# Expert weights of a mixture-of-experts layer loaded in 16 KB runs per partition, with strided column reads on the other side

## The chip, the cores and the metric

The kernel runs on one core of a Trainium2 chip. The metric is the device time of one execution in microseconds (us), taken as the median of several runs. A core has five engines with instruction queues of their own: PE (TensorE, matrix products; PEld is its weight load, which runs beside the products), DVE (VectorE), ACT (ScalarE), POOL (GpSimd) and SP (SyncE, which here issues DMAs). Sixteen DMA engines carry data between HBM and the on-chip memory SBUF, which has 128 partitions.

## The reference

Two transformer blocks in fp32 on 256 tokens of width 1024. The first block has a mixer (RWKV-7 heads and block attention), then a mixture of 32 experts with top 4 of 32; the second block has attention, a projection and a dense feed-forward. What matters here is the expert layer of the first block:

```
logits = h @ w_router + b_router            # h = rms_norm(x, norm2_g) * (1 + scale2) + shift2
top_val, top_idx = lax.top_k(logits, 4);  weights = softmax(top_val)
for each expert e and the tokens that chose it (xb = h[tok]):
    gu   = xb @ w_gate_up[e] + b_gate_up[e]             # 1024 x 2048
    gate = min(gu[:, :1024], 7);  up = clip(gu[:, 1024:], -7, 7)
    act  = (up + 1) * gate * sigmoid(1.702 * gate)
    y    = act @ w_down[e] + b_down[e]                  # 1024 x 1024
x = x + gate2 * (sum over the experts of weight * y)
```

Each expert has 8 MB of w_gate_up and 4 MB of w_down, all of it read once: 32 x 12 MB.

## The kernel before, in words

The kernel has three stages. **Stage one** (`phase1`, L249) computes the conditioning rows (w_ada), the mixer, w_out and the router. Near its end `choose` (L913) transposes the residual `xm` in 128-column slices (L922), multiplies it by the router's weights `wr` (already scaled by `sc2` at L629) and finds each token's four experts. **Stage two** (`experts`, L1064) goes through the 32 experts. **Stage three** (`phase3`, L1250) is the second block.

In stage two an expert takes at most 64 tokens. Experts go in pairs: `gather` (L1091) builds one-hot matrices `s` for two experts and multiplies them with `xm`, eight slices of 128 columns by two halves of the tokens (L1108, the slice of `xm` is the stationary operand, which PEld loads); the result, scaled and shifted by columns of `sc2` and `sh2`, is `xe`, the gathered tokens with the model dimension on the partitions. `gate_up` (L1129) multiplies `xe` by the weights, `down` (L1151) transposes the activations in four 128-column slices (L1157, the slice of `act` is the stationary operand) and multiplies them by w_down; `combine` (L1173) adds the pair to the residual. PE runs the operations of this stage in the written order (class `InOrder`), so a gather of the next pair stands between gate_up and down of an odd expert.

The weights come as chunks of 2 MB, six per expert (`issue`, L1046): four of w_gate_up (two blocks of 128 rows each, of 2048 floats) and two of w_down (four blocks of 128 rows, of 1024 floats). Row p of a block goes to partition p:

```
g = A["w_gate_up"][e].rearrange("(k p) f -> p k f", p=128)
w = self.stream(g[:, 2 * j:2 * j + 2], 2, 2048, pool)
```

so a partition's part of a w_gate_up chunk is two runs of 8 KB, and of a w_down chunk four runs of 4 KB. All chunks are issued on SP's queue in order. There are nine slots of 16 KB per partition for them (`self.slots`); SP waits for the slot's last reader on PE and then issues. The first nine chunks are issued during stage one, which ends while they land. The last chunk of all is issued as four pieces of 512 KB.

The columns that `gather`, `choose` and `down` slice must match the rows that a partition holds: slice k of `xm` has the model dimensions that partition p of block k multiplies. `sc2` (from norm2_g, which comes with the small vectors at the start, and the conditioning rows through `ada_col`, L314), `sh2` and `wr` have the same order. For the last expert `cuts` (L1125) divides the work between gate_up and down into two halves of 256 columns, so that the first half's transposes start early. A branch for experts with more than 64 tokens (`overflow`, L973) is not taken with these inputs.

Of the kernel before, what the change touches and what calls it, by code (L numbers as in the profile page):

```python
# [88 lines left out]


CST_A, CST_B = _consts()


class InOrder:
# [20 lines left out]
class Kernel:  # L115
# [133 lines left out]
    def phase1(self):  # L249
# [61 lines left out]
            PE.matmul(ps, self.k("ones"), gacc[:, q], start=True, stop=True)  # L311
            return ps

        def ada_col(r, i0):  # L314

            ps = self.psum("adac")
            for j in range(4):
                PE.matmul(ps[:, 4 * j:4 * j + 4], r[:, j * 128:(j + 1) * 128], self.k("sel32")[:, i0:i0 + 4], start=True,
                          stop=True, skip_group_check=True)
            return ps[:, 0:16].rearrange("p (j i) -> p i j", i=4)  # L320

# [292 lines left out]

        wr = p1.tile([128, 8, NE], F32, tag="wr", name="wr")
        cvec = self.W[:, 0]
        with tc.issue_after(self.last_dma):
            nc.sync.dma_start(wr, A["w_router"].rearrange("(k p) e -> p k e", p=128))
            nc.sync.dma_start(cvec, A["b_router"].partition_broadcast(128))
        pv = ada_col(r1, 6)  # L620
        sc2, sh2 = self.sc2, self.sh2
        DVE.tensor_scalar(ic(sc2), pv[:, 2:4], 1.0, None, op0=OP.add)
        DVE.tensor_tensor(sc2, sc2, self.v("g2"), op=OP.mult)
        DVE.tensor_copy(ic(sh2), pv[:, 0:2])
        ps = self.psum("cv")
        for k in range(8):
# [286 lines left out]
    def choose(self, a, wrs, cvec):  # L913

        nc = self.nc
        PE, ACT, DVE = nc.tensor, nc.scalar, nc.vector
        x1, rs, ident, pr = self.xm, self.rs, self.k("ident"), self.prp
        x1T = pr.tile([128, 8, 128], F32, tag=f"x1T{a}", name="x1T")
        for k in range(0, 8, 4):
            ps = self.psum("x1t", chain=k > 3)  # L920
            for kk in range(4):
                PE.transpose(ps[:, kk * 128:(kk + 1) * 128], x1[:, a, (k + kk) * 128:(k + kk + 1) * 128], ident)  # L922
            o = ps.rearrange("p (a b) -> p a b", a=4)
            if k:
                ACT.activation(x1T[:, k:k + 4], o, AF.Copy)
            else:
                DVE.tensor_copy(x1T[:, k:k + 4], o)
        mask = self.mask[:, a]
        ps = self.psum("lg")
        for k in range(8):  # L930
            PE.matmul(ps[:, 0:NE], x1T[:, k], wrs[:, k], start=k == 0, stop=k == 7)
        lg = pr.tile([128, NE], F32, tag=f"lg{a}", name="lg")
        DVE.scalar_tensor_tensor(lg, ps[:, 0:NE], rs[:, a:a + 1], cvec, op0=OP.mult, op1=OP.add)
        m8 = pr.tile([128, 8], F32, tag=f"m8{a}", name="m8")
        DVE.max(m8, lg)
        ng = pr.tile([128, 2], F32, tag=f"ng{a}", name="ng")
        DVE.tensor_scalar(ng[:, 0:1], m8[:, 0:1], -1.0, None, op0=OP.mult)
        DVE.memset(m8[:, 4:8], BIG)
        zap = pr.tile([128, NE], F32, tag=f"zap{a}", name="zap")
        DVE.match_replace(zap, m8, lg, -BIG)  # L940
        DVE.tensor_tensor(mask, lg, zap, op=OP.not_equal)
        self.lgs = getattr(self, "lgs", []) + [(lg, ng)]
# [30 lines left out]
    def overflow(self):  # L973
# [4 lines left out]
        with tc.If(self.most > CAP):  # L978
            with tc.tile_pool(name="pof", bufs=1) as pool:
# [3 lines left out]
                with tc.For_i(0, NE, 1) as e:  # L983
# [5 lines left out]
                    def turned(normed):  # L989
                        for k in range(8):  # L990
                            ps = self.psum("ot")
                            PE.transpose(ps[:, 0:128], act[:, k * 128:(k + 1) * 128], ident)
                            if normed:
                                DVE.tensor_scalar(t8[:, k], ps[:, 0:128], self.sc2[:, k:k + 1], self.sh2[:, k:k + 1],
                                                  op0=OP.mult, op1=OP.add)
                            else:
                                DVE.tensor_copy(t8[:, k], ps[:, 0:128])
# [6 lines left out]
                    for a in range(2):  # L1004
                        DVE.tensor_scalar(act, xm[:, a], self.rs[:, a:a + 1], None, op0=OP.mult)
                        turned(True)
                        for i in range(2):
                            pg = [self.psum("og") for _ in range(2)]
                            for k in range(8):
                                for j in range(2):  # L1010
                                    c = slice(j * D + i * 512, j * D + (i + 1) * 512)
                                    w = weights("w_gate_up", slice(k * 128, (k + 1) * 128), c)
                                    PE.matmul(pg[j], t8[:, k], w, start=k == 0, stop=k == 7)
                            b = pool.tile([128, 2, 512], F32, tag="b", name="bo")
                            for j in range(2):
                                c = slice(j * D + i * 512, j * D + (i + 1) * 512)
                                nc.sync.dma_start(b[:, j], A["b_gate_up"][ds(e, 1), c].partition_broadcast(128))
                            g, u, s = b[:, 0], b[:, 1], act[:, i * 512:(i + 1) * 512]
                            DVE.tensor_tensor(g, pg[0], g, op=OP.add)
                            DVE.tensor_scalar(g, g, 7.0, None, op0=OP.min)  # L1020
                            DVE.tensor_tensor(u, pg[1], u, op=OP.add)
                            DVE.tensor_scalar(u, u, 7.0, -7.0, op0=OP.min, op1=OP.max)
                            ACT.activation(s, g, AF.Sigmoid, scale=1.702)
                            DVE.scalar_tensor_tensor(u, u, 1.0, g, op0=OP.add, op1=OP.mult)
                            DVE.tensor_tensor(s, s, u, op=OP.mult)
                        turned(False)
                        py = [self.psum("oy") for _ in range(2)]
                        for k in range(8):
                            for i in range(2):
                                w = weights("w_down", slice(k * 128, (k + 1) * 128), slice(i * 512, (i + 1) * 512))  # L1030
                                PE.matmul(py[i], t8[:, k], w, start=k == 0, stop=k == 7)
                        for i in range(2):
                            hs = slice(i * 512, (i + 1) * 512)
                            y = pool.tile([128, 512], F32, tag="y", name="oyy")
                            DVE.scalar_tensor_tensor(y, py[i], we[:, a:a + 1], self.gate2[:, hs], op0=OP.mult,
                                                     op1=OP.mult)
                            DVE.tensor_tensor(x1[:, a, hs], x1[:, a, hs], y, op=OP.add)
# [8 lines left out]
    def issue(self, upto):  # L1046

        A = self.A
        while self.issued < min(upto, 6 * self.ne):
# [2 lines left out]

            pool = self.slot(i, lambda p: e < self.ne - 1 or p is not self.ring)
            if j < 4:
                g = A["w_gate_up"][e].rearrange("(k p) f -> p k f", p=128)
                w = self.stream(g[:, 2 * j:2 * j + 2], 2, 2048, pool)
            else:
                d = A["w_down"][e].rearrange("(k p) f -> p k f", p=128)
                w = self.stream(d[:, 4 * j - 16:4 * j - 12], 4, 1024, pool, 4 if i == 6 * self.ne - 1 else 1)
            self.chunks[i] = w  # L1060
            self.issued += 1
            self.last_chunk = self.last_dma
# [1 line left out]
    def experts(self):  # L1064
# [26 lines left out]
        def gather(e):  # L1091
# [12 lines left out]
            for kk in range(0, 8, 4):  # L1104
                ps = self.psum("ga")
                for k in range(4):
                    for a in range(2):
                        PE.matmul(ps[:, k * 128:(k + 1) * 128], xm[:, a, (kk + k) * 128:(kk + k + 1) * 128], s[:, a],  # L1108
                                  start=a == 0, stop=a == 1, skip_group_check=True)
                for k in range(4):  # L1110
                    g, b = self.sc2[:, kk + k:kk + k + 1], self.sh2[:, kk + k:kk + k + 1]
# [12 lines left out]

        def cuts(e):  # L1125

            return [slice(0, 256), slice(256, 512)] if e == ne - 1 else [slice(0, 512)]

        def gate_up(e, ws):  # L1129
            xe = st[e & ~1][0][:, :, 64 * (e & 1):64 * (e & 1) + 64]  # L1130
# [11 lines left out]
                        PE.matmul(p[64 * h:64 * h + 64, :], xe[:, k], w[:, k % 2, c:c + 512], start=False, stop=k == 7)  # L1142
            u, s = (pool.tile([128, 512], F32, tag=n, name=n, bufs=1) for n in ("u", "sg"))
            for c in cuts(e):
                ACT.activation(s[:, c], pg[:, c], AF.Sigmoid, scale=1.702)  # L1145
                DVE.tensor_scalar(u[:, c], pu[:, c], 8.0, -6.0, op0=OP.min, op1=OP.max)  # L1146
                DVE.scalar_tensor_tensor(u[:, c], pg[:, c], 7.0, u[:, c], op0=OP.min, op1=OP.mult)
                DVE.scalar_tensor_tensor(u[:, c], s[:, c], SIG_MAX, u[:, c], op0=OP.min, op1=OP.mult)
            return u

        def down(e, act, ws):  # L1151
            at = pool.tile([128, 4, 2, 64], F32, tag="at", name="at")
            for c in cuts(e):
                ps = self.psum("at")
                js = slice(c.start // 128, c.stop // 128)
                for j in range(js.start, js.stop):
                    PE.transpose(ps[:, j * 128:(j + 1) * 128], act[:, j * 128:(j + 1) * 128], ident)  # L1157
                ACT.activation(at[:, js], ps[:, c].rearrange("p (j h s) -> p j h s", h=2, s=64), AF.Copy)  # L1158
            py = self.psum("py")
            for c in range(2):  # L1160
                for j in range(4):
# [446 lines left out]
```

## Time and profile before

| | us |
|---|---|
| median of 3 runs | 1568.0 (1567.0 to 1577.03) |
| the profiled execution | 1568.55 |
| its span, first to last instruction | 1566.8 |
| PE busy in the span | 1414.5 (90%) |
| DMA: bytes, mean rate | 505.15 MB, 322 GB/s |

The profiled execution is 0.55 us above the median. Its own time is 1.75 us more than its span; the rows below are all of that execution, with times in us from the start of the span. A busy PE is not a PE at its peak: a chunk's products come late when its data comes late. The page cuts the span into 40 slices of 39 us. Stage one fills the first seven of them, stage two ends in the 32nd, and stage three takes the rest.

### The profile page before, as it was taken

The page shows a single profiled execution, that of the slowest core. Times are in us where ns is not written, and L with a number is a line of the kernel's source. Part 1 is how long each engine was busy: PE and PEld are TensorE (multiplying, and loading weights), DVE is VectorE, ACT ScalarE, POOL GpSimd, SP SyncE. Part 2 cuts the span into 40 slices and gives each one's busy share as a digit, 9 for nine tenths or more (in the row PEclk, how much of TensorE's full clock was granted, in tenths as well). Part 3 has the DMA queues.
Part 4 walks back from the last instruction along what each step waited for, and adds up shares of the span by engine and source line. Part 5 has one row for each costly group of instructions (what it writes and reads, how often), then busy time and mean ns, then how long its engine had stood idle before and what let it go on. Part 6 is the DMA issues. An engine that isn't in the chain of part 4 may idle for free. (4 is left out here: it accounts for less than half of the span.)

```text
span 1566.8 us, 19105 instructions
## 1 busy us (share of the span) xinstructions
PE 1414.5 (90%) x7818; PEld 804.6 (51%) x7818; DVE 572.1 (37%) x1145; ACT 394.5 (25%) x767; POOL 212.9 (14%) x190
## 2 busy tenths in 40 slices
PE   5999999899999988888788889999888899899996
PEld 2976777433343333233233234433332597699995
DVE  3575877313122221122122122221211345565445
ACT  4862335101010000000010011100100366455553
POOL 1243661000000000000000000000000233252221
PEclk9998999899999999999999999999999999999998
DMA  9734747899999999999999999999999741525440
GB/s 335 262 118 148 265 166 285 339 419 415 418 418 416 416 418 417 416 417 419 416 416 418 416 413 416 417 418 416 418 417 417 285 162 54 215 108 202 175 162 28
DMA packets 115061, 505.15 MB, mean 322 GB/s; under 512 B 5548, under 2 KB 6572, under 8 KB 82168
## 3 DMA queue, kind: packets, MB, share of 16 engines
q1 hardware_dynamic: 114792, 503.74, 80.9%
q8 instruction: 63, 1.03, 0.3%
q14 instruction: 30, 0.25, 0.0%
q0 software_dynamic: 176, 0.14, 0.0%
HBM read 502.81 MB, written 1.05 MB: 322 GB/s over the span
## 5 line engine op out<-in xcount | busy, mean ns | idle before, releaser
L109 PE MATMUL pg<-w,xe 128*64 128x512 f32 x1024 | 271.2, 600 | 65.9 <-DMA w<-w_gate_up 65.9
L109 PE MATMUL pu<-w,xe 128*64 128x512 f32 x1024 | 267.5, 592 | 0.0
L109 PE MATMUL py<-w,at 128*64 128x512 f32 x1024 | 232.1, 606 | 23.1 <-ACT at L1158 20.6
L1146 DVE TENSOR_SCALAR u<-pu 128x512 f32<-128x512 f32 (+1 forms) x33 | 22.2, 675 | 477.0 <-PE pu L109 477.0
L1145 ACT ACTIVATE sg<-pg 128x512 f32<-128x512 f32 (+1 forms) x33 | 19.3, 584 | 690.7 <-PE pg L109 689.0
L109 PEld LDWEIGHTS pg<-w,xe 128*64 128x64 f32 x1024 | 70.0, 137 | 217.5 <-issue 112.0
L109 PEld LDWEIGHTS py<-w,at 128*64 128x64 f32 x1024 | 72.3, 139 | 161.6 <-issue 133.3
L109 PEld LDWEIGHTS pu<-w,xe 128*64 128x64 f32 x1024 | 75.5, 137 | 145.8 <-issue 145.6
L140 ACT ACTIVATE w3h<-w 128x512 fp32r<-128x512 f32 x184 | 115.4, 631 | 110.8 <-PE d L1299 59.4
L141 DVE TENSOR_TENSOR w3l<-w,w3h 128x512 fp32r<-128x512 f32 x132 | 96.8, 739 | 113.3 <-ACT w3h L140 108.5
L141 POOL TENSOR_TENSOR w3l<-w,w3h 128x512 fp32r<-128x512 f32 x52 | 67.3, 1299 | 430.4 <-ACT w3h L140 419.2
L1170 DVE TENSOR_TENSOR y<-py,gate 64x512 f32<-64x512 f32 x64 | 44.1, 689 | 209.4 <-PE py L109 208.7
L1298 PE MATMUL d<-xh,w3h 128*128 128x256 f32 x352 | 100.3, 287 | 0.9 <-ACT xh L1285 0.9
L1299 PE MATMUL d<-xl,w3h 128*128 128x256 f32 x352 | 100.8, 287 | 0.1
L1300 PE MATMUL d<-xh,w3l 128*128 128x256 f32 x352 | 100.5, 287 | 0.0
L1234 POOL TENSOR_TENSOR wml<-w,wml 128x512 fp32r<-128x512 f32 x4 | 5.1, 1278 | 695.1 <-ACT wml L1233 695.1
L1298 PEld LDWEIGHTS d<-xh,w3h 128*128 128x128 f32 x352 | 68.6, 196 | 1.6 <-ACT xh L1285 1.3
L1299 PEld LDWEIGHTS d<-xl,w3h 128*128 128x128 f32 x352 | 68.8, 195 | 0.6 <-DVE xl L1287 0.4
L1300 PEld LDWEIGHTS d<-xh,w3l 128*128 128x128 f32 x352 | 68.6, 195 | 0.2 <-DVE w3l L141 0.2
L109 PEld LDWEIGHTS ga<-s,xm 128*128 128x128 f32 x512 | 60.5, 197 | 13.5 <-issue 11.9
L109 PE MATMUL ga<-s,xm 128*128 128x128 f32 x512 | 63.6, 284 | 1.2 <-DVE s L1098 1.2
L109 PE MATMUL cb<-y,swt 128*128 128x512 f32 x128 | 59.2, 605 | 0.8 <-DVE y L1170 0.8
(421 smaller groups left out, 2041.1 us busy)
## 6 DMA issues: line engine op xcount, KB each, us to landing
w<-w_gate_up SPq DMA_DIRECT2D x128, 2048.0 KB, 24.9
w<-w_down SPq DMA_DIRECT2D x71, 2048.0 KB, 30.6
w<-w_ada SPq DMA_DIRECT2D x12, 2048.0 KB, 8.2
w<-w_up SPq DMA_DIRECT2D x8, 2048.0 KB, 7.6
w<-w_in SPq DMA_DIRECT2D x6, 2048.0 KB, 13.1
w<-w_in_sb SPq DMA_DIRECT2D x5, 2048.0 KB, 11.7
w<-w_out SPq DMA_DIRECT2D x4, 2048.0 KB, 7.7
w<-w_mem_kv SPq DMA_DIRECT2D x1, 2048.0 KB, 31.5
```

What stands on the lines that cost most here:

```text
L109: return self._keep(self.tc.nc.tensor.matmul(*a, **k))
L140: self.nc.scalar.activation(hi, src, AF.Copy)
L141: eng.tensor_tensor(lo, src, hi.bitcast(F32), op=OP.subtract)
L1145: ACT.activation(s[:, c], pg[:, c], AF.Sigmoid, scale=1.702)
L1146: DVE.tensor_scalar(u[:, c], pu[:, c], 8.0, -6.0, op0=OP.min, op1=OP.max)
L1170: DVE.tensor_tensor(st[e & ~1][2][r, hs], py[64 * h:64 * h + 64], self.gate2[64 * h:64 * h + 64, hs], op=OP.mult)
L1234: (POOL if k % 2 else DVE).tensor_tensor(wl, w[:, k], wh.bitcast(F32), op=OP.subtract)
L1298: PE.matmul(o, wh[:, ws], xh[:, k], start=k == 0 and i % 2 == 0, stop=False, skip_group_check=True)
L1299: PE.matmul(o, wh[:, ws], xl[:, k], start=False, stop=False, skip_group_check=True)
L1300: PE.matmul(o, wl[:, ws], xh[:, k], start=False, stop=k == 7, skip_group_check=True)
```

## The change: which row of the weights goes to which partition

Each partition now takes consecutive rows: two rows of w_gate_up (16 KB in one run) or four rows of w_down (16 KB in one run). The tokens' columns keep their order in SBUF. Slice k of the model dimension therefore becomes every second column of a 256-column block (`by_run`), and slice j of the activations every fourth column of a 512-column block; gather, the router's transposes and the transposes of the activations read these strided columns. norm2_g and w_router are loaded in the same order by four small DMAs each, on SP's queue behind the last conditioning weights, where one DMA of w_router stood; norm2_g goes straight into `sc2`, so that two DVE operations become one. The halves of the last expert become strided too. The last chunk still comes in four pieces of one row per partition.

```diff
+def by_run(k):
+    return slice(256 * (k // 2) + k % 2, 256 * (k // 2) + 256, 2)
...
-        def ada_col(r, i0):
+        def ada_col(r, i0, cols=lambda j: slice(j * 128, (j + 1) * 128)):
...
-                PE.matmul(ps[:, 4 * j:4 * j + 4], r[:, j * 128:(j + 1) * 128], self.k("sel32")[:, i0:i0 + 4], start=True,
+                PE.matmul(ps[:, 4 * j:4 * j + 4], r[:, cols(j)], self.k("sel32")[:, i0:i0 + 4], start=True,
...
+        sc2, sh2 = self.sc2, self.sh2
         with tc.issue_after(self.last_dma):
-            nc.sync.dma_start(wr, A["w_router"].rearrange("(k p) e -> p k e", p=128))
+            for c in range(4):
+                r = slice(256 * c, 256 * c + 256)
+                nc.sync.dma_start(wr[:, 2 * c:2 * c + 2], A["w_router"][r].rearrange("(p k) e -> p k e", k=2))
+                nc.sync.dma_start(sc2[:, 2 * c:2 * c + 2], A["norm2_g"][r].rearrange("(p k) -> p k", k=2))
             nc.sync.dma_start(cvec, A["b_router"].partition_broadcast(128))
-        pv = ada_col(r1, 6)
-        sc2, sh2 = self.sc2, self.sh2
-        DVE.tensor_scalar(ic(sc2), pv[:, 2:4], 1.0, None, op0=OP.add)
-        DVE.tensor_tensor(sc2, sc2, self.v("g2"), op=OP.mult)
+        pv = ada_col(r1, 6, by_run)
+        DVE.scalar_tensor_tensor(ic(sc2), pv[:, 2:4], 1.0, ic(sc2), op0=OP.add, op1=OP.mult)
...
-                PE.transpose(ps[:, kk * 128:(kk + 1) * 128], x1[:, a, (k + kk) * 128:(k + kk + 1) * 128], ident)
+                PE.transpose(ps[:, kk * 128:(kk + 1) * 128], x1[:, a, by_run(k + kk)], ident)
...
-                g = A["w_gate_up"][e].rearrange("(k p) f -> p k f", p=128)
-                w = self.stream(g[:, 2 * j:2 * j + 2], 2, 2048, pool)
+                g = A["w_gate_up"][e][256 * j:256 * (j + 1)].rearrange("(p k) f -> p k f", k=2)
+                w = self.stream(g, 2, 2048, pool)
             else:
-                d = A["w_down"][e].rearrange("(k p) f -> p k f", p=128)
-                w = self.stream(d[:, 4 * j - 16:4 * j - 12], 4, 1024, pool, 4 if i == 6 * self.ne - 1 else 1)
+                d = A["w_down"][e][512 * (j - 4):512 * (j - 3)].rearrange("(p k) f -> p k f", k=4)
+                w = self.stream(d, 4, 1024, pool, 4 if i == 6 * self.ne - 1 else 1)
...
-                        PE.matmul(ps[:, k * 128:(k + 1) * 128], xm[:, a, (kk + k) * 128:(kk + k + 1) * 128], s[:, a],
+                        PE.matmul(ps[:, k * 128:(k + 1) * 128], xm[:, a, by_run(kk + k)], s[:, a],
...
-            return [slice(0, 256), slice(256, 512)] if e == ne - 1 else [slice(0, 512)]
+            return [slice(0, 2), slice(2, 4)] if e == ne - 1 else [slice(0, 4)]
+        cut = lambda t, c: t.rearrange("p (q j) -> p q j", j=4)[:, :, c] if c != slice(0, 4) else t
...
-                ACT.activation(s[:, c], pg[:, c], AF.Sigmoid, scale=1.702)
+                ACT.activation(cut(s, c), cut(pg, c), AF.Sigmoid, scale=1.702)
...
-                    PE.transpose(ps[:, j * 128:(j + 1) * 128], act[:, j * 128:(j + 1) * 128], ident)
+                    PE.transpose(ps[:, j * 128:(j + 1) * 128], act[:, j:512:4], ident)
```

The three DVE operations behind the sigmoid take `cut` in the same way, and the branch that is not taken reads its rows and columns in the new order.

## Rows read from the trace of the kernel before

**Rows 1.** The page's slices: TensorE's clock, DMA busy share in tenths, and GB/s.
```profile
PEclk9998999899999999999999999999999999999998
DMA  9734747899999999999999999999999741525440
GB/s 335 262 118 148 265 166 285 339 419 415 418 418 416 416 418 417 416 417 419 416 416 418 416 413 416 417 418 416 418 417 417 285 162 54 215 108 202 175 162 28
```

**Rows 2.** Stretches: length, engines' busy us (instructions), TensorE's clock, DMA share, GB/s.
```profile
284.00:292.00 8.00, 8.00 (x46) 3.46 (x46) 4.21 (x14) 2.47 (x4) 0.00 (x0) 1.00 0.24 69
292.00:300.00 8.00, 7.49 (x36) 2.23 (x32) 0.45 (x1) 0.60 (x1) 0.00 (x0) 1.00 1.00 403
300.00:1180.00 880.00, 793.47 (x3836) 313.55 (x3838) 193.74 (x394) 73.99 (x154) 5.11 (x4) 0.99 1.02 417
1220.00:1228.00 8.00, 7.56 (x30) 2.51 (x30) 0.51 (x2) 0.77 (x2) 0.00 (x0) 0.79 1.04 392
```

**Rows 3.** Waits from 300 to 1225: us in total, times, longest us.
```profile
PE pg L109 <- DMA w<-w_gate_up: 65.9, 59, 1.7
PE py L109 <- ACT at L1158: 20.6, 30, 0.7
```

**Rows 4.** PE in order of time: start, us, operation, [idle before it <- what ended that].
```profile
560.96 0.65 PE L109 MATMUL pg<-w,xe 128*64 128x512 f32 x2 [0.43 <-DMA w<-w_gate_up]
...
621.11 1.08 PE L109 MATMUL pg<-w,xe 128*64 128x512 f32 x4 [0.41 <-DMA w<-w_gate_up]
...
626.08 0.65 PE L109 MATMUL pg<-w,xe 128*64 128x512 f32 x2 [1.32 <-DMA w<-w_gate_up]
...
863.62 1.08 PE L109 MATMUL pg<-w,xe 128*64 128x512 f32 x4 [0.41 <-DMA w<-w_gate_up]
...
868.59 0.65 PE L109 MATMUL pg<-w,xe 128*64 128x512 f32 x2 [1.32 <-DMA w<-w_gate_up]
```

**Rows 5.** Chunks issued about 1209: issue ns, first and last start; then landing times.
```profile
L133 SPq DMA_DIRECT2D w<-w_in_sb x2: 1767/5627/9487, 1209.6 to 1211.4; - x2
L133 SPq DMA_DIRECT2D w<-w_down x1: 4237/4237/4237, 1205.2 to 1205.2; - x1
...
DMA to landing us min/median/max: 19.3/20.3/23.8
```

**Rows 6.** The page's weight loads and products of all gathers: busy us, mean ns.
```profile
L109 PEld LDWEIGHTS ga<-s,xm 128*128 128x128 f32 x512 | 60.5, 197 | 13.5 <-issue 11.9
L109 PE MATMUL ga<-s,xm 128*128 128x128 f32 x512 | 63.6, 284 | 1.2 <-DVE s L1098 1.2
```

**Rows 7.** PEld from 300 to 1225: the transposes' loads of the activations.
```profile
L112 PEld LDWEIGHTS at<-ca,u 128*128 128x128 f32 x128 | 15.3, 141 | 14.4 <-DVE u L1148 7.5 <-issue 7.0
```

**Rows 8.** PE in order of time: a router transpose, the first gather, a later one.
```profile
270.09 0.65 PE L922 MATMUL x1t<-ca,xm 128*128 128x128 f32 x4
...
278.75 5.88 PE L109 MATMUL ga<-s,xm 128*128 128x128 f32 x32 [1.22 <-DVE s L1098]
...
604.57 3.84 PE L109 MATMUL ga<-s,xm 128*128 128x128 f32 x32
```

**Rows 9.** SP's queue in order of time, from 176 to 195.
```profile
176.68 0.58 SPq L618 DMA_DIRECT2D wr<-w_router  x1
177.31 3.08 SPq L619 DMA_DIRECT2D W<-b_router  x1
189.98 0.37 SPq L133 DMA_DIRECT2D w<-w_out  x1
```

**Rows 10.** PE's products with w_out's weights: ns min/median/max, first and last start us.
```profile
L877 PE MATMUL wo<-wsh,yoh x32: 389/389/501, 236.3 to 265.6; 128*128 128x512 f32 x32
```

**Rows 11.** The router's constant row, from 172 to 200 in order of time.
```profile
186.34 1.97 PE L627 MATMUL cv<-wr,sh 128*128 128x32 f32 x16
```

**Rows 12.** ACT and DVE about the last expert, in order of time.
```profile
1217.19 0.38 ACT L1145 ACTIVATE sg<-pg 128x256 f32<-128x256 f32 x1 [24.55 <-PE pg L109]
...
1218.79 0.42 DVE L1147 SCALAR_TENSOR_TENSOR u<-pg,u 128x256 f32<-128x256 f32 x1
```

More of the change, by code (lines that the diff above doesn't have):

```diff
@@ L991, in turned @@
                             ps = self.psum("ot")
-                            PE.transpose(ps[:, 0:128], act[:, k * 128:(k + 1) * 128], ident)
+                            c = by_run(k) if normed else slice(k * 128, (k + 1) * 128)
+                            PE.transpose(ps[:, 0:128], act[:, c], ident)
                             if normed:
@@ L1011, in overflow @@
                                     c = slice(j * D + i * 512, j * D + (i + 1) * 512)
-                                    w = weights("w_gate_up", slice(k * 128, (k + 1) * 128), c)
+                                    w = weights("w_gate_up", by_run(k), c)
                                     PE.matmul(pg[j], t8[:, k], w, start=k == 0, stop=k == 7)
@@ L1144, in gate_up @@
             for c in cuts(e):
-                ACT.activation(s[:, c], pg[:, c], AF.Sigmoid, scale=1.702)
-                DVE.tensor_scalar(u[:, c], pu[:, c], 8.0, -6.0, op0=OP.min, op1=OP.max)
-                DVE.scalar_tensor_tensor(u[:, c], pg[:, c], 7.0, u[:, c], op0=OP.min, op1=OP.mult)
-                DVE.scalar_tensor_tensor(u[:, c], s[:, c], SIG_MAX, u[:, c], op0=OP.min, op1=OP.mult)
+                ACT.activation(cut(s, c), cut(pg, c), AF.Sigmoid, scale=1.702)
+                DVE.tensor_scalar(cut(u, c), cut(pu, c), 8.0, -6.0, op0=OP.min, op1=OP.max)
+                DVE.scalar_tensor_tensor(cut(u, c), cut(pg, c), 7.0, cut(u, c), op0=OP.min, op1=OP.mult)
+                DVE.scalar_tensor_tensor(cut(u, c), cut(s, c), SIG_MAX, cut(u, c), op0=OP.min, op1=OP.mult)
             return u
@@ L1154, in down @@
                 ps = self.psum("at")
-                js = slice(c.start // 128, c.stop // 128)
-                for j in range(js.start, js.stop):
-                    PE.transpose(ps[:, j * 128:(j + 1) * 128], act[:, j * 128:(j + 1) * 128], ident)
-                ACT.activation(at[:, js], ps[:, c].rearrange("p (j h s) -> p j h s", h=2, s=64), AF.Copy)
+                for j in range(c.start, c.stop):
+                    PE.transpose(ps[:, j * 128:(j + 1) * 128], act[:, j:512:4], ident)
+                ACT.activation(at[:, c], ps[:, c.start * 128:c.stop * 128].rearrange("p (j h s) -> p j h s", h=2, s=64),
+                               AF.Copy)
             py = self.psum("py")
```

## The prediction, made before the changed kernel was run

> **What bounds the kernel now.** I read the page's slices first. The DMA engines are full from the ninth slice to the 31st, at 413 to 419 GB/s, and nowhere else for long [rows 1]. That is stage two. The stretches say the same: 417 GB/s and a DMA share of 1.02 over 880 us, while PE, though busy 793 of 880, waits [rows 2]. For what it waits stands in the table of waits: 65.9 us for w_gate_up [rows 3]. So stage two lasts as long as its weights take to come in, and PE has some 66 us to spare in it.
>
> Where does this stretch begin? At 284 to 292 the DMA engines stand nearly idle (69 GB/s), at 292 to 300 they are full [rows 2]. The nine slots hold the first nine chunks, and the tenth goes out when PE has used the first. So what delays the end of stage one delays everything; from there to the last chunk the time is the sum of the chunks' transfers; behind it comes a tail and stage three, which the change leaves alone.
>
> What does one chunk take? PE's waits for w_gate_up end when a chunk has landed. Two successive chunks: 621.11 and 626.08, or 863.62 and 868.59; both times 4.97 us [rows 4]. From 560.96 to 621.11 are two experts, 60.15 us, so 30.08 for one [rows 4]. Less four chunks of w_gate_up (19.88) that leaves 10.20 for two of w_down: **5.10 us**. (Ten experts, 560.96 to 863.62, give 30.27 each: now and then something else comes between; I leave that as it is.) Both chunks are 2 MB, so the difference lies in how the bytes are cut: 16 runs of 8 KB for each of the 16 DMA engines against 32 of 4 KB. A third point lies behind the stage: two chunks of w_in_sb, in runs of 2 KB (64 per engine), issued at 1209.6 and 1211.4, landed 20.3 and 23.8 us later (the 19.3 of that view is a piece of w_down), at 1229.9 and 1235.2: 5.3 us [rows 5]. The three lie near one line: (5.10 - 4.97)/16 = 8.1 ns per run, and (5.3 - 5.1)/32 = 6 ns with an error of some 3.
>
> **The change part by part.**
>
> *Runs of 16 KB.* Each engine then has 8 runs per chunk. No row shows weights in such runs. On the line a chunk takes 4.97 - 8 x 0.0081 = 4.905 us. The lower bound is the line's value at no cost per run, 4.97 - 16 x 0.0081 = 4.84; the upper bound, with no gain beyond 8 KB, is 4.97. I take the line: it holds from 2 KB to 8 KB, and 16 KB is one more step of the same kind. After the ninth chunk there are 183 in the full stretch: 121 of w_gate_up, 62 of w_down, of which the last still comes in pieces of 4 KB. The gain is 121 x 0.065 + 61 x 0.195 = 7.9 + 11.9 = **19.8 us**; between the bounds, 121 x 0 + 61 x 0.13 = 7.9 and 121 x 0.13 + 61 x 0.26 = 31.6. It is on the path in full as long as PE still waits: 65.9 less 19.8 leaves 46 us of waiting. What is late next is then the same chunk, earlier. SP isn't in the way: it issues a chunk some 20 us ahead of its landing [rows 5].
>
> The Trainium skill (DMA: Bandwidth & Descriptors, Why small descriptors are slow) speaks against this part: it gives a fixed cost of about three cycles per packet, which it says matters at 256 bytes or less. With its 850 MHz that is 3.5 ns per run, and the sum by it would be 121 x 8 x 3.5 ns + 61 x 24 x 3.5 ns = 8.5 us of gain, an estimate; the rows show more than twice its price per run, and I go by the rows.
>
> *Strided slices in gather.* The stationary operand `xm` is read with a step of 8 bytes. No PE operand of the kernel before that I cost here has a step, so the nearest rows are the same loads without one: 197 ns for a load of 128 columns by its record, and 3.84 us for the 32 products of one gather, 0.12 us per load and product [rows 6, 8]. Bounds per load: nothing (the load runs beside the product before it), and one more 0.12 if loads take twice as long. A gain is excluded, since a strided read fetches no less. I take nothing, the value of the rows as they are. In the full stretch, 480 of the 512 loads of gathers [rows 6] have PE's waits as cover; at 0.12 they would add 57.6 us and eat the 46 that are left. The first gather (5.88 us [rows 8]) has no cover: up to 32 x 0.12 = 3.8 us.
>
> *Transposes in choose.* 16 loads, four in 0.65 us [rows 8], on the way to the first gather: nothing, or 16 x 0.12 = 1.9 us.
>
> *Transposes of the activations.* 128 loads of 141 ns [rows 7], now with a step of 16 bytes: nothing, or 0.14 each; 124 of them under PE's waits (17.4 us at most), the last expert's four in the tail (0.6 us at most). Here the Trainium skill (SBUF — State Buffer, Door 1) has a rule that fits: a line of SBUF is 16 bytes and needs two hits for full rate, so a step of two fp32 is free and a step of four is not. By it only these loads grow, under cover, and the sum keeps its value but for the tail's 0.6; no run so far shows a strided load.
>
> *The last expert's halves.* ACT and DVE read and write 128x256 in pairs with a step: two halves of four operations, about 0.4 us each [rows 12], some ten with the copies, in a row behind the last w_gate_up chunk. Nothing at least, 4 us if each doubles. I take 0.3: the same elements in the same number of operations.
>
> *The small loads in stage one.* One DMA of w_router (0.58 us to issue) becomes eight. Between 0.37 and 0.58 each [rows 9], that is 2.4 to 4.1 us more on SP's queue. Behind them stand b_router (to 180.39) and then w_out at 189.98, which waits for its slot: 9.6 us of cover [rows 9]. If each took b_router's 3.08, w_out would go out 14 us late; its first product is at 236.3 [rows 10]. On PE the row `cv` needs the whole of `wr`, at 186.34 [rows 11]; what comes 2.4 to 4.1 us later there can hold up PE, and with it the products of the solve queued behind. `sc2` now waits for norm2_g as well, and DVE with it, if the order written out puts it early; the fused operation saves 0.16 us off the path. Bounds: nothing, and 4 us. I take 1, as most of the 4 is covered.
>
> **Sum.** 1568.55 (the profiled execution) - 19.8 + 0.3 + 1.0 = 1550.05. The median of the runs is 0.55 below that execution, so the forecast is **1549.5**.
>
> **The rivals.**
>
> *No step beyond 8 KB.* Either a 16 KB run is cut again on its way, or the per-run cost of the rows belongs to runs under 8 KB. Then w_gate_up stays at 4.97 and w_down falls to it: 7.9 us, less 1.3 of costs: 1568.0 - 6.6 = **1561.4**. For it: only three sizes lie on the line, and the third only roughly. Against it: from 4 to 8 KB the slope had not bent. The skill's price per packet, named above, ends at 1568.0 - 8.5 + 1.3 = 1560.8, an estimate, and so beside this case.
>
> *PE becomes the bound: slower.* A strided load takes longer than PE can hide. Place: the 480 loads of the gathers and 124 of the transposes in the full stretch, and 48 (first gather and choose) ahead of it. With x us more per load, the change is -19.8 + 1.3 + 48x + (604x - 46 if positive); it crosses zero at 652x = 64.5, x = 0.099 us. At 0.12 (loads twice as long, by the gather's pace) it is +13.7, **1582**; at the load's own 0.19 [rows 6], +59, 1627. For it: the pace of a gather is that of its loads, so nothing but PE's waits hides them. Against it: a step of 8 bytes is the smallest there is, and it would have to double.
>
> *Hidden anyway.* The gain comes in, but stage one loses as much as its bounds allow (4 + 3.8 + 1.9) and the tail 4: 1568.0 - 19.8 + 13.7 = 1562. It needs all four ends at once and is the least likely of these.
>
> **How the numbers follow.** A measurement of this kernel can tell about 1% from no change, here 15.7 us: below 1552.3 is faster, above 1583.7 slower. The line: 0.62, with its own range of 1538 to 1556 (gain of 31.6 to about 14), of which I put 0.52 under 1552.3 and 0.10 above. No step beyond 8 KB: 0.20. PE the bound: 0.12, of which 0.09 ends beyond 1%. Hidden anyway: 0.06. So faster 0.52; same 0.10 + 0.20 + 0.03 + 0.06 = 0.39; slower 0.09. The range reaches from 1541 over the second case to 1565: it leaves out the PE case (0.12) and the outermost of the line's low end (0.04).
>
> **What would show it.** Successive waits for w_gate_up end 4.90 us apart and two experts take 58.9 (12 x 4.905) instead of 60.15; 428 GB/s in the full stretch; half as many packets, and PE waiting some 46 us for w_gate_up. Chunks of w_gate_up still at 4.97 speak for the second case; PE's wait near nothing, with gathers over 5 us, for the third. The forecast is wrong at its root if chunks of 16 KB runs take longer than 5.01, the mean of the two kinds now: then runs of this length cost, which no row excludes.

## The result, and the profile after

The changed kernel takes **1544.45 us** (median of 5 runs, 1542.83 to 1553.07), beside 1568.29 us for the kernel before on the same chip. The ratio is 0.9845, with a 95% interval of 0.9821 to 0.987: 23.8 us less. The forecast was 1549.5, 18.5 less, in a range of 1541 to 1565.

The rows here are of a second profiled execution of the changed kernel (1543.47 us, span 1541.7, against 1568.55 and 1566.8 before). In the first, of 1553.07 us, TensorE's granted clock fell to 0.50 (1.2 GHz) in stage one, after a stretch in which PE was busy for 2.44 of 4.00 us (170 to 174). It stood there from 178 to 200, where the second has 1.00 (2.4 GHz). Why it fell stays open: the kernel before was busy for 2.29 of 4.00 us from 174 to 178 and kept 1.00. As runs of the kernel before lie as far apart (1567.0 to 1577.03), I take the fall as no part of the change.

The page's slices, of the same three kinds as in [rows 1], and the line on packets:

```profile
PEclk9998999899999999999999999999999999999998
DMA  9833746899999999999999999999999741535440
GB/s 338 269 110 142 262 163 285 343 428 428 427 428 427 429 428 427 428 428 428 427 428 427 424 423 428 428 428 428 428 427 425 257 157 54 218 116 213 164 165 28
DMA packets 74599, 505.17 MB, mean 328 GB/s; under 512 B 5661, under 2 KB 6685, under 8 KB 50025
```

The full stretch is the same stretch, at 423 to 429 GB/s where [rows 1] have 413 to 419. The kernel before had 115061 packets on its page; 40462 are gone. The runs that the change saves are 128 chunks x 8 x 16 engines + 63 x 24 x 16 = 40576; the small loads bring 114 packets more. Of those that are left, 74599 - 50025 = 24574 are of 8 KB or more, and the runs of 16 KB are (128 + 63) x 8 x 16 = 24448. So a run of 16 KB is one packet here: it is not cut again on its way. The prediction expected half as many packets; of the chunks' own 38% are left, of the whole page's 65%.

The same stretches as in [rows 2] (length, busy us and instructions of PE, PEld, DVE, ACT and POOL, TensorE's clock, DMA share, GB/s):

```profile
284.00:292.00 8.00, 8.00 (x43) 2.97 (x43) 3.65 (x13) 2.33 (x4) 0.00 (x0) 1.00 0.34 94
292.00:300.00 8.00, 6.69 (x32) 1.97 (x28) 1.15 (x2) 0.60 (x1) 0.00 (x0) 1.00 1.01 428
300.00:1180.00 880.00, 814.41 (x3924) 328.56 (x3926) 199.26 (x402) 75.86 (x156) 5.09 (x4) 0.99 1.01 427
1196.00:1204.00 8.00, 7.18 (x34) 2.85 (x36) 1.21 (x3) 1.12 (x3) 0.00 (x0) 1.00 1.04 392
```

The DMA engines are as full as before and move 427 GB/s instead of 417. PE does 3924 instructions in the 880 us where it did 3836, more than two in a hundred more, because the weights come sooner. The last row is the end of stage two, 24 us ahead of its partner in [rows 2], and at the full clock, where that one has 0.79.

The table of waits from 300 to 1225 (us in total, times, longest), to be read beside [rows 3]:

```profile
PEld pg L114 <- DMA w<-w_gate_up: 63.0, 41, 2.2
PE pg L114 <- DMA w<-w_gate_up: 41.8, 35, 1.3
```

PE still waits for w_gate_up, 24 us less than before. Its queue of weight loads, PEld, waits for the same tile longer, as the upper row shows; before, that row had 96.2 us. All of PE's waits for weights lie behind 585 us: from 300 to 585 the table has none. That will matter below.

PE in order of time (start, us, operation, [idle before it <- what ended that]), as in [rows 4]:

```profile
617.12 1.08 PE L114 MATMUL pg<-w,xe 128*64 128x512 f32 x4 [0.78 <-DMA w<-w_gate_up]
622.10 1.08 PE L114 MATMUL pg<-w,xe 128*64 128x512 f32 x4 [1.33 <-DMA w<-w_gate_up]
646.47 1.08 PE L114 MATMUL pg<-w,xe 128*64 128x512 f32 x4 [1.24 <-DMA w<-w_gate_up]
651.37 1.08 PE L114 MATMUL pg<-w,xe 128*64 128x512 f32 x4 [1.25 <-DMA w<-w_gate_up]
...
654.96 4.04 PE L114 MATMUL ga<-s,xm 128*128 128x128 f32 x32
...
680.84 1.08 PE L114 MATMUL pg<-w,xe 128*64 128x512 f32 x4 [1.33 <-DMA w<-w_gate_up]
...
705.23 1.08 PE L114 MATMUL pg<-w,xe 128*64 128x512 f32 x4 [1.25 <-DMA w<-w_gate_up]
```

From 646.47 to 651.37 is one chunk, 4.90 us. From 622.10 to 680.84, and from 646.47 to 705.23, are two experts: 58.74 and 58.76 us (60.15 in [rows 4]). Eight chunks of w_gate_up and four of w_down share them, so one of w_down takes (58.75 - 8 x 4.90)/4 = 4.89: both kinds now take the same. The gather between them lasts 4.04 us where [rows 8] have 3.84.

**Where the time went**, by the two profiled executions: from the tenth chunk's issue to the last landing 935.3 us before (289.24 to 1224.50) and 912.5 after (288.44 to 1200.97), so -22.7; ahead of it -0.8; behind it 342.3 and 340.7, so -1.5. Together -25.1, the difference of the spans.

### The profile page after: what moved, and what is told of

It reads as the page before. It is cut to its first block, busy times and chain, and to the rows that moved or that the text cites. A ratio compares the mean times of both kernels' runs of the same rounds, so it can differ in the third digit from the quotient of the medians.

```text
span 1551.3 us, 19123 instructions
## 1 busy us (share of the span) xinstructions
PE 1425.1 (92%) x7818; PEld 824.2 (53%) x7818; DVE 570.8 (37%) x1144; ACT 396.5 (26%) x767; POOL 213.0 (14%) x190
## 2 busy tenths in 40 slices
DMA packets 74599, 505.17 MB, mean 326 GB/s; under 512 B 5661, under 2 KB 6685, under 8 KB 50025
## 5 line engine op out<-in xcount | busy, mean ns | idle before, releaser
L114 PE MATMUL py<-w,at 128*64 128x512 f32 x1024 | 228.8, 599 | 23.8 <-ACT at L1167 20.6
L145 ACT ACTIVATE w3h<-w 128x512 fp32r<-128x512 f32 x184 | 115.4, 631 | 108.6 <-PE d L1309 57.8
```

Of the source, the lines that this page charges most:

```text
L114: return self._keep(self.tc.nc.tensor.matmul(*a, **k))
L145: self.nc.scalar.activation(hi, src, AF.Copy)
```

## The experiments

Two theories stood against each other. **Runs:** the time of a chunk goes by the number of runs alone, at some 8 ns for each run of an engine, and the strided reads that the new order asks for cost nothing. **Its rivals:** it is the other partition and address order that helps, not the length; or 16 KB is no better than 8 KB and only w_down gained; or a run costs less than half of that and something else gave the rest; or strided reads do cost and the loads give back more than they show. In reads only, runs only, short runs and step 8 below, the channels that a product reads in its columns are no longer those of the rows of its weights; instructions, sizes and transfers are as named. Each kernel was timed in turns with the kernel before.

**The changed kernel once more**, for a second profile.

> The changed kernel once more, for a second profile. If the lower clock of TensorE about 175 to 202 us in the first profile is not part of the change, the span is some 1541 to 1543 us, stage two starts issuing its tenth chunk at about 289 us as before the change (289.2) and not at 298, and chunks land 4.90 us apart. If it is part of the change: 1551 and 298 again.

Measured: 1544.22 us, ratio 0.9852 (0.9817 to 0.9887). It is the profile shown above.

**w_gate_up alone in 16 KB runs.** The changed kernel with w_down as it was:

```diff
-d = A["w_down"][e][512 * (j - 4):512 * (j - 3)].rearrange("(p k) f -> p k f", k=4)
-w = self.stream(d, 4, 1024, pool, 4 if i == 6 * self.ne - 1 else 1)
+d = A["w_down"][e].rearrange("(k p) f -> p k f", p=128)
+w = self.stream(d[:, 4 * j - 16:4 * j - 12], 4, 1024, pool, 4 if i == 6 * self.ne - 1 else 1)
```

With it come the cuts, halves and transposes of the kernel before.

> Only w_gate_up comes in 16 KB runs (with gather, router and small loads in that order); w_down keeps four runs of 4 KB and the contiguous transposes. A cost per run that holds up to 16 KB: w_gate_up chunks 4.90 us apart, w_down 5.11, 121 x 0.07 = 8.5 us faster, 1560. No step beyond 8 KB: w_gate_up stays at 4.97 and the time at 1568.

Measured: 1558.43 us, ratio 0.9945 (0.9926 to 0.9964). PE in order of time:

```profile
586.22 1.08 PE L114 MATMUL pg<-w,xe 128*64 128x512 f32 x4 [0.56 <-DMA w<-w_gate_up]
591.12 1.08 PE L114 MATMUL pg<-w,xe 128*64 128x512 f32 x4 [1.25 <-DMA w<-w_gate_up]
...
645.94 1.08 PE L114 MATMUL pg<-w,xe 128*64 128x512 f32 x4 [0.56 <-DMA w<-w_gate_up]
```

Two experts take 59.72, a chunk of w_gate_up 4.90; that leaves (59.72 - 39.20)/4 = 5.13 for one of w_down, the old value. The step from 8 to 16 KB is worth 9.5 us by itself (1567.94 for the kernel before in these rounds). The rival "no step beyond 8 KB" allowed it nothing and falls.

**w_down alone in 16 KB runs.** The kernel before with the changed kernel's load of w_down, its `cuts` and halves and its strided transposes:

```diff
-d = A["w_down"][e].rearrange("(k p) f -> p k f", p=128)
-w = self.stream(d[:, 4 * j - 16:4 * j - 12], 4, 1024, pool, 4 if i == 6 * self.ne - 1 else 1)
+d = A["w_down"][e][512 * (j - 4):512 * (j - 3)].rearrange("(p k) f -> p k f", k=4)
+w = self.stream(d, 4, 1024, pool, 4 if i == 6 * self.ne - 1 else 1)
...
-PE.transpose(ps[:, j * 128:(j + 1) * 128], act[:, j * 128:(j + 1) * 128], ident)
+PE.transpose(ps[:, j * 128:(j + 1) * 128], act[:, j:512:4], ident)
```

> Only w_down comes in 16 KB runs, with the transposes at a step of four columns and the last expert's strided halves; w_gate_up, gather, router and small loads as before. A cost per run: w_down chunks 4.90 us apart, 61 x 0.21 = 12.8 us faster, 1555.5. If the whole gain lies in w_down: 1545.

Measured: 1551.50 us, ratio 0.9894 (0.9858 to 0.9931). PE in order of time:

```profile
587.57 1.08 PE L109 MATMUL pg<-w,xe 128*64 128x512 f32 x4 [0.21 <-DMA w<-w_gate_up]
592.53 1.08 PE L109 MATMUL pg<-w,xe 128*64 128x512 f32 x4 [1.31 <-DMA w<-w_gate_up]
...
646.89 1.08 PE L109 MATMUL pg<-w,xe 128*64 128x512 f32 x4 [0.23 <-DMA w<-w_gate_up]
```

Here w_gate_up keeps 4.96, two experts take 59.32, and w_down falls to (59.32 - 39.68)/4 = 4.91. The gain is 16.4 us, and 9.5 + 16.4 = 25.9 is close to the 23.7 of both together in the same rounds: the two parts add up, within what the intervals leave open.

**The strided reads without the long runs.** The changed kernel with both loads of the kernel before:

```diff
-g = A["w_gate_up"][e][256 * j:256 * (j + 1)].rearrange("(p k) f -> p k f", k=2)
-w = self.stream(g, 2, 2048, pool)
+g = A["w_gate_up"][e].rearrange("(k p) f -> p k f", p=128)
+w = self.stream(g[:, 2 * j:2 * j + 2], 2, 2048, pool)
```

and w_down loaded as in the diff of w_gate_up alone.

> The weights come in the runs of before, all strided reads and the small loads are those of the change, so that weights meet the wrong columns (the expert layer's numbers differ). Strided reads under cover: 1567 to 1570, PE's waits for w_gate_up about as before (66 us) less what the loads take. If strided loads matter: later than 1570, and PE's waits well under 60 us. If part of the 24 us came from the new order in stage one: 1563 or less.

Measured: 1568.31 us, ratio 0.9992 (0.9973 to 1.0011).

**The long runs without the strided reads.** The kernel before with both loads of the changed one (the same lines the other way round).

> The weights come in 16 KB runs, everything else is as before: contiguous reads, one DMA of w_router, norm2_g with the small vectors (weights meet the wrong columns, the expert layer's numbers differ). If the runs are the whole of it: 121 x 0.07 + 61 x 0.21 = 21 us faster, 1547, within 3 us of the changed kernel. If the strided reads and small loads cost something: faster than the changed kernel by that.

Measured: 1544.23 us, ratio 0.9848 (0.9832 to 0.9865), the changed kernel's own time. The waits of the two kernels for w_gate_up:

```profile
PE pg L114 <- DMA w<-w_gate_up: 61.1, 55, 1.7
```

```profile
PE pg L109 <- DMA w<-w_gate_up: 44.9, 37, 1.3
```

The first row is reads only: the strided reads and the small loads take 5 of the 65.9 us of waiting [rows 3], and no time that shows (4.2 us less to 1.7 more by the interval). The second is runs only: the loads take 21 us of waiting away, and the 23.8 us come from them alone.

**Shorter runs still.** The kernel before with w_gate_up in runs of 2 KB and w_down in runs of 1 KB (64 and 128 for each engine and chunk):

```diff
-g = A["w_gate_up"][e].rearrange("(k p) f -> p k f", p=128)
-w = self.stream(g[:, 2 * j:2 * j + 2], 2, 2048, pool)
+g = A["w_gate_up"][e][256 * j:256 * (j + 1)].rearrange("r (c f) -> (r c) f", f=512)
+w = self.stream(g.rearrange("(k p) f -> p k f", p=128), 8, 512, pool).rearrange("p (a b) f -> p a (b f)", a=2)
```

and w_down likewise, as 16 rows of 256 columns.

> The same 2 MB chunks, each read as runs of 2 KB (w_gate_up, 64 per DMA engine) and 1 KB (w_down, 128), laid out otherwise, so the expert layer's numbers differ; reads as before. At 8.1 ns per run: w_gate_up 5.36 us apart, w_down 5.88, 121 x 0.39 + 62 x 0.78 = 95 us slower, 1663. At the price per packet that the Trainium skill gives (3.5 ns): 41 us slower, 1609.

Measured: 1677.16 us, ratio 1.07 (1.0682 to 1.0718). PE in order of time:

```profile
587.82 1.08 PE L109 MATMUL pg<-w,xe 128*64 128x512 f32 x4 [1.33 <-DMA w<-w_gate_up]
593.25 1.08 PE L109 MATMUL pg<-w,xe 128*64 128x512 f32 x4 [1.77 <-DMA w<-w_gate_up]
...
621.53 1.08 PE L109 MATMUL pg<-w,xe 128*64 128x512 f32 x4 [1.31 <-DMA w<-w_gate_up]
```

A chunk of w_gate_up takes 5.43, one expert 33.71, so one of w_down (33.71 - 4 x 5.43)/2 = 6.0. Now there are five points. The medians of the intervals between successive landings in stage two, some 80 to 90 of w_gate_up and some 40 of w_down in each kernel (16 KB from the changed kernel, 8 and 4 KB from the kernel before, 2 and 1 KB from this one):

| run | runs per engine and chunk | us per 2 MB chunk | ns per run, from the row above |
|---|---|---|---|
| 16 KB | 8 | 4.895 | |
| 8 KB | 16 | 4.970 | 9.4 |
| 4 KB | 32 | 5.113 | 8.9 |
| 2 KB | 64 | 5.421 | 9.6 |
| 1 KB | 128 | 6.014 | 9.3 |

It is one straight line of 9.3 ns per run, with 4.82 us at no run at all. Against the kernel before, this kernel should lose 121 x 0.451 + 62 x 0.901 = 110.4 us by the table; it lost 109.1 (1568.05 in these rounds). The table's lower rows are of this very kernel, so that tests the sum and not the price. The prediction's own 8.1 ns gave 95 us, to 1663. At the 3.5 ns per packet that the prediction drew from the Trainium skill (DMA: Bandwidth & Descriptors, Why small descriptors are slow), an estimate, it would have lost 41 us, to 1609; the row disagrees.

**The order of the changed kernel, in the runs of the kernel before.** Each row of weights goes where the changed kernel puts it, but a chunk of w_gate_up comes in two transfers of 8 KB runs, one of w_down in four of 4 KB. Beside it the kernel before, cut into transfers in the same way (two and four).

```diff
-w = self.stream(g, 2, 2048, pool)
+w = self.stream(g, 2, 2048, pool, 2)
...
-w = self.stream(d, 4, 1024, pool, 4 if i == 6 * self.ne - 1 else 1)
+w = self.stream(d, 4, 1024, pool, 4)
```

> The changed kernel with each chunk issued one row per partition at a time: w_gate_up as two DMAs of 1 MB, w_down as four of 512 KB, so that partitions hold consecutive rows as in the change but the runs are 8 and 4 KB as before. If the number of runs counts: 4.97 and 5.11 us per 2 MB, 1568. If it counts which partition reads which address: 4.90, 1545.

> The kernel before with the same division, w_gate_up in two DMAs and w_down in four: a control for the number of DMAs. If more DMAs cost nothing, as the four pieces of the last chunk suggest (1.28 us each): 1568. If they do, the excess is to be taken off the run with consecutive rows.

Measured: 1566.05 us, ratio 0.9984 (0.9972 to 0.9996), for the order; 1567.36 us, ratio 1.0011 (0.9985 to 1.0037), for the cut. Their full stretches, the order first, then the cut:

```profile
300.00:1180.00 880.00, 807.68 (x3842) 317.11 (x3844) 194.59 (x394) 74.67 (x154) 5.11 (x4) 0.99 1.02 417
```

```profile
300.00:1180.00 880.00, 804.95 (x3848) 310.13 (x3848) 192.89 (x393) 74.05 (x154) 5.09 (x4) 1.00 1.02 417
```

Both move 417 GB/s, as the kernel before does. Which partition gets which address is worth some 2 us beside the kernel before (0.6 to 4.4 by the interval) and 1.3 beside the cut; two to four times as many transfers cost nothing that shows, at most some 6 us by the interval. Neither comes near the 23.8. What counts is the length of a run.

**A wider step.** The changed kernel, in which all gathers but the first read `xm` with a step of 32 bytes instead of 8. It asks how near the rival "PE becomes the bound" was.

```diff
-PE.matmul(ps[:, k * 128:(k + 1) * 128], xm[:, a, by_run(kk + k)], s[:, a],
+PE.matmul(ps[:, k * 128:(k + 1) * 128], xm[:, a, slice(kk + k, D, 8) if e else by_run(kk + k)], s[:, a],
```

> The changed kernel, with all gathers but the first reading every eighth column (a step of 32 bytes; the slices then don't match the weights' rows, so the expert layer's numbers differ). By the Trainium skill's rule on lines of 16 bytes (SBUF, Door 1) such a load costs what the transposes' step of 16 bytes costs: loads of about 205 ns in place of 197. If the pace of a gather follows that, 4.04 us becomes 4.4 to 6, 5 to 30 us of PE work in all, below the 42 us that PE still waits: 1544, no change in time. If strided loads cannot hide: up to 1574.

Measured: 1550.72 us, ratio 0.9884 (0.9859 to 0.991). PEld's loads of the gathers from 300 to 1225 (busy us, mean ns), in the changed kernel and then in this one:

```profile
L114 PEld LDWEIGHTS ga<-s,xm 128*128 128x128 f32 x480 | 57.8, 197 | 12.2 <-issue 10.5 <-PE pg L114 1.6
```

```profile
L114 PEld LDWEIGHTS ga<-s,xm 128*128 128x128 f32 x480 | 115.5, 335 | 12.2 <-issue 10.5 <-PE pg L114 1.6
```

And one gather of it on PE, in order of time:

```profile
617.13 7.89 PE L114 MATMUL ga<-s,xm 128*128 128x128 f32 x32
```

A gather takes 7.89 us instead of 4.04: this is the doubling that the rival needed, at four times the step. Both expectations missed, the 4.4 to 6 us of a gather and the 1544 of the whole. It adds 15 x 3.85 = 57.8 us of PE's work, and 6.5 us come out.

**Every gather twice.** The changed kernel, in which all gathers but the first do their products a second time. The second pass begins each sum anew.

```diff
-for a in range(2):
+for a in (0, 1, 0, 1) if e else (0, 1):
```

> The changed kernel, with the products of all gathers but the first done twice (same result): what loads of twice the length would cost PE. It adds 15 x 4.04 = 60.6 us of PE work to stage two. If PE's 42 us of waits for w_gate_up pay for it in full before the rest shows, as the third rival was priced: 18.6 us slower, 1563. If only the waits of the expert with the gather pay (half of them): 40 us slower, 1584. If PE has more room than its waits show: under 1555.

Measured: 1552.07 us, ratio 0.9891 (0.9865 to 0.9917). A gather takes 7.80 us, so 15 x 3.76 = 56.4 us more, and 7.9 come out. (The profile is of an execution of 1561.16 us, in which the clock fell in stage one as in the first of the changed kernel; the rows are of stage two.) The waits for w_gate_up, and then the full stretch:

```profile
PEld pg L114 <- DMA w<-w_gate_up: 9.5, 6, 2.6
PE pg L114 <- DMA w<-w_gate_up: 6.5, 5, 1.7
```

```profile
300.00:1180.00 880.00, 849.45 (x4346) 380.56 (x4344) 194.23 (x394) 75.65 (x155) 5.09 (x4) 0.99 1.00 424
```

Two quite different ways to make PE slower agree: with some 57 us more work, 424 GB/s instead of 427. By PE's 41.8 us of waiting, 15 us would have come out. Nor are the 6.5 us what was left when all cover was spent. These are two stretches of the kernel with the step of 32 bytes:

```profile
310.00:440.00 130.00, 126.79 (x558) 54.07 (x555) 29.39 (x58) 9.29 (x19) 0.00 (x0) 0.97 0.97 407
440.00:1180.00 740.00, 716.52 (x3286) 325.26 (x3282) 162.60 (x333) 65.12 (x135) 5.09 (x4) 1.00 1.01 427
```

The changed kernel moves 428 and 427 GB/s in them. So nearly the whole loss lies in the first 130 us (21 of 428 GB/s are 6.4 us of them), and from 440 on the extra work costs nothing. PE's own pace tells why. These are its gathers, one for each two experts, in the changed kernel and then in the one with the step of 32 bytes:

```profile
385.92 4.04 PE L114 MATMUL ga<-s,xm 128*128 128x128 f32 x32
...
438.57 4.04 PE L114 MATMUL ga<-s,xm 128*128 128x128 f32 x32
...
491.22 4.04 PE L114 MATMUL ga<-s,xm 128*128 128x128 f32 x32
```

```profile
326.70 7.88 PE L114 MATMUL ga<-s,xm 128*128 128x128 f32 x32
...
391.14 7.89 PE L114 MATMUL ga<-s,xm 128*128 128x128 f32 x32
...
447.64 7.89 PE L114 MATMUL ga<-s,xm 128*128 128x128 f32 x32
...
504.14 7.88 PE L114 MATMUL ga<-s,xm 128*128 128x128 f32 x32
```

In the changed kernel PE starts the stage behind the first nine chunks, which have landed, and waits for no weights until 585. While it works these off, it takes 52.65 us for two experts, 6.1 less than the 58.74 of their transfers. That is its room: 15 x 6.1, some 91 us over the stage, an estimate. With the step of 32 bytes it takes 56.50, which is still less than 58.74. Only the first interval there is longer, 64.44 us; the granted clock stood at 0.50 (1.2 GHz) from 372 to 376 in it. With every gather twice it takes 56.42, behind a first interval of 64.36. In that first interval the DMA engines ran short, it seems because slots came free too late.

## Why the prediction was right, step by step

**What bounds the kernel** held: stage two lasts as long as its transfers, and PE's waits were no part of the path but a part of the room beside it. Runs only shows it most plainly: it changes nothing but the two loads, and gets the whole gain.

**Runs of 16 KB** was right in its mechanism and undersized in its price. The sum took 8.1 ns per run; it is 9.3. The larger part of the fault is in the second point of the line: 5.10 us for a w_down chunk was what two experts left over, and the landings themselves give 5.113, or 8.9 ns. At 4.895 for both kinds, the term is 121 x (4.970 - 4.895) + 61 x (5.113 - 4.895) = 9.1 + 13.3 = 22.4 us instead of 19.8; the profiles show 22.7. That the line went on to 16 KB, the step that was chosen and not read, is borne out by w_gate_up alone.

**The rule that spoke against this part** fell. The table shows 9.3 ns per run, and a line that is as steep from 8 to 16 KB as from 1 to 2. The rule of the Trainium skill (DMA: Bandwidth & Descriptors, Why small descriptors are slow), about three cycles per packet and joining packets worth it only at 256 bytes or less, doesn't agree with that: the 3.5 ns, an estimate from those cycles, are some 2.7 times too little here, and the cost matters at sizes far above that bound.

**Strided slices.** The gathers in the full stretch take 4.04 us for 3.84 [rows 8], 3 us in all and in PE's room, as taken. Their loads, from 300 to 1225, took this before:

```profile
L109 PEld LDWEIGHTS ga<-s,xm 128*128 128x128 f32 x480 | 54.8, 192 | 12.2 <-issue 10.6 <-PE pg L109 1.6
```

So they take 197 ns for 192. The first gather, which had no cover, takes 5.83 us for 5.88 [rows 8], and the router's transposes 0.75 us for four instead of 0.65, some 0.3 us in all. The activations' transposes, with a step of 16 bytes, show their step in the record:

```profile
L117 PEld LDWEIGHTS at<-ca,u 128*128 128x128 f32 x128 | 19.1, 205 | 13.5 <-DVE u L1158 7.5 <-issue 5.9
```

That is 205 ns for 141 [rows 7], 3.8 us in all, and hidden too. The loads thus grew by 5 ns at a step of 8 bytes and by 64 at 16. The Trainium skill (SBUF — State Buffer, Door 1) has lines of 16 bytes that want two hits, from which the prediction took it that a step of two fp32 is free and a step of four is not; but for the 5 ns, these two rows agree. A third, in the experiment with a step of 32 bytes, is not told by it: each element has a line of its own there as at 16 bytes, and the load of a gather grew by 143 ns, from 192 to 335. The row at 16 bytes is of other loads, so how much of the difference is the step no run tells.

**The small loads** were given 1.0 us and cost none that shows. SP's queue (start, us to issue), to be read beside [rows 9]:

```profile
175.86 0.57 SPq L626 DMA_DIRECT2D wr<-w_router  x1
176.49 0.42 SPq L627 DMA_DIRECT2D sc<-norm_g  x1
...
184.71 0.33 SPq L627 DMA_DIRECT2D sc<-norm_g  x1
185.08 0.43 SPq L628 DMA_DIRECT2D W<-b_router  x1
189.44 0.38 SPq L138 DMA_DIRECT2D w<-w_out  x1
```

The small loads, b_router the last of them, end 5.1 us later (185.51 for 180.39), more than the 4.1 that were reckoned, since SP stands from 179.4 to 184.7 before the last `sc`; yet w_out goes out at 189.44, where [rows 9] have 189.98. The cover named, 9.6 us, was enough. `cv` begins at 187.45, 1.1 us later than in [rows 11], and the tenth chunk goes out 0.8 us earlier nevertheless (288.44 for 289.24).

**The last expert's halves** were given 0.3 us. The stretch behind the last landing is 1.5 us shorter, but not for a reason of the change. Its longest products:

```profile
1197.76 7.09 PE L114 MATMUL py<-w,at 128*64 128x512 f32 x32
```

Before they took 8.78 us, at a granted clock of 0.79 [rows 2]: after 1218 to 1220, in which PE was busy for 0.27 of 2.00 us, it stood at 0.50 (1.2 GHz) for some three. That goes to and fro between kernels with the same work there: the order in old runs has 7.09, the cut 8.37, w_down alone 8.79. So the 1.5 of the 25.1 us between the two profiles are that clock's, and whether the halves cost a tenth or three is below what the runs can tell.

**The rivals.** No step beyond 8 KB: 4.90 us per chunk, and 9.5 us for w_gate_up alone, rule it out. PE becomes the bound: the break-even of 0.099 us per load was far above the 5 ns that a gather's load grew, and above the 64 ns of the transposes' loads. Its price was also too high. It took the 46 us of PE's waits for the room, where PE's pace gives some 91 (an estimate, as above), and already the 66 us "to spare" were too few: before the change two experts took PE 52.38 us (384.66 to 437.04, without a wait) beside 60.15 of transfers. At 0.12 us per load it gave 1582 of the whole, where the step of 32 bytes ended at 1550.72 (in the gathers of the full stretch alone: 11.6 us reckoned, 6.5 measured, and those at the start of the stage). Hidden anyway: not one of its four ends came.

**The sum again**, from the forecast's -18.5 to the -25.1 between the two profiles: 2.9 more from the runs, 1.8 in stage one (1.0 reckoned and 0.8 gained, which is no more than two executions differ by), 1.8 behind the last landing (0.3 reckoned, 1.5 of the clock); the rest is rounding. Between the medians it is -23.8, and the runs' term alone is 22.4 of that. No two errors of the sum cancelled, so the forecast lay in its range by the right mechanism and not by luck; 1544.45 is also under the 1552.3 from which the prediction counted the kernel as faster, at 0.52.

No run here beats the changed kernel clear of the noise. On the line, the 8 runs that are left in a chunk are 74 ns, or 13.6 us over 183 chunks, and that is the most that longer runs could still give; they weren't tried, as a slot holds 16 KB per partition.

## What to carry to other kernels

Where the DMA engines are full for long, count the runs that a transfer falls into, not its bytes alone: a rearrangement that gives each partition neighbouring rows makes the run longer at no other cost than a step in the columns that PE reads, and a step of two fp32 is nearly free. Take the price of a run from two sizes in the trace, by the intervals between landings rather than by what other sums leave over. The room of PE beside a full DMA is better read from its pace in a stretch where it doesn't wait (52.65 us for two experts here, beside 58.74 of transfers) than from the sum of its waits. When added work does move the time, look in which stretch it was lost before calling the room spent.

## What the runs showed that I had not expected

The cost of a run is the same, 8.9 to 9.6 ns, over a range of 16 in size, up to 16 KB: in this range there is no size from which it is nothing, only one from which it is small (74 ns of 4.895 us at 16 KB, 1.19 of 6.01 at 1 KB). The line without runs, 2 MB in 4.82 us, is 435 GB/s. The Trainium skill (DMA: Bandwidth & Descriptors, Where 436 GB/s comes from) gives that number as the ceiling of the 16 ports; the line agrees, though no run reaches it (427 GB/s in the full stretch).

PE had far more room than its waits had shown: some 91 us by its pace (an estimate) for 41.8 of waits. For the first third of the stage it works off chunks that have landed, so that it waits for no weights although it is faster than the transfers. Behind that it waits some 4.8 us for two experts (24.2 from 585 to 880) and not 6.1; a product's end is modelled in these records, so part of its waiting may look busy, which no run here settles. From 440 on, two kernels with 3.8 us more work for two experts lost nothing that shows.

A step of 32 bytes made the weight loads of the gathers 143 ns longer and one of 16 bytes those of the transposes 64 ns, in loads of 128 columns; whether it goes on so was not tried.
